# Second layer: pairs from tile 2 on and to the end, combined activations directly behind the norm, squares beside the pairs

## The chip, the core and the metric

The kernel runs on one core of one Trainium2 chip. The metric is the device time of one execution in microseconds (us). Engines are named as the profile names them: PE (TensorE matmuls), PEld (TensorE weight loads, beside PE), DVE (VectorE), ACT (ScalarE), POOL (GpSimd) and SP (SyncE, which here only starts transfers). Each engine works through its own instructions in order; an instruction that waits for another engine holds up everything behind it on its own.

## What is computed

A trunk of two layers over 1024 tokens of 1024 channels, all in fp32. The first layer mixes tokens by a convolution, the second by trailing means (pool); each is followed by a SwiGLU feed-forward part (FFN) with 2816 hidden channels. Cut to what matters:

```python
def swiglu_ffn(h, w_gate, w_up, w_down):
    return (jax.nn.silu(h @ w_gate) * (h @ w_up)) @ w_down

for i in range(DEPTH):                       # DEPTH = 2
    h = modulate(rms_norm(x, norm_mix_g[i]), sh_m, sc_m)
    y = conformer_conv(...) if i % 2 == 0 else multiscale_pool(...)
    x = x + (1.0 + g_m)[:, None, :] * y
    h = modulate(rms_norm(x, norm_ffn_g[i]), sh_f, sc_f)
    y = swiglu_ffn(h, ffn_w_gate[i], ffn_w_up[i], ffn_w_down[i])
    x = x + (1.0 + g_f)[:, None, :] * y
return rms_norm(x, final_g)
```

## The kernel before

**Tiling.** Tokens are split into two chunks of 512, A (tiles named x_0_*) and B (x_1_*), with channels on the 128 partitions, so x of a chunk is 8 tiles of 128x512. The hidden channels of the FFN are 22 tiles of 128 (NF = 22), called f-tiles. fp32 products are made from high and low parts: `hhi`/`hlo` for activations, a cast for the high part and the remainder for the low one, and weights in the same way; each product is three matmuls (high·high, high·low, low·high).

**Plain f-tiles** (`ffn_p1`): gate and then up of one f-tile, 8 × 3 = 24 matmuls of 512 columns each. **Downs** (`ffn_p2`): for two f-tiles, 8 output tiles of 6 matmuls, each added to x by DVE (`update`).

**Pairs** (`ffn_pair`, L1133): gate (or up) of two f-tiles at once, in the manner of Strassen, with 7 quarter products where the plain way has 8. Each is a `quad` of 12 matmuls of 256 columns. Four quads use weights or activations that are sums: the weight sums s1 to s4 (`Pair.prepare`; cast to `shi` and `slo` tiles) and the activation sums t1 to t4 (`combined`; `thi` and `tlo`), called T. A pair unit writes two PSUM banks: bank a takes quads w11, s2, s3 and w22 one on top of the other in its left half, bank e takes s1 and s4 in its right and w12 in its left half. Since the running sum in a is needed at three stages, ACT copies it away after w11 and again after s2, and the next quad into a waits for that copy. In all but the first pair of a stage, four slots of downs of the pair before it (6 matmuls of 512 columns each) stand between the quads. The core of the unit:

```python
quad(a[:, :H], w11, b11, True)
S_.copy(r[:, LEFT], a[:, :H])
quad(right, s1, t1, True)
S_.copy(q[:, RIGHT], right)
down()
quad(a[:, :H], s2, t2, False)
S_.copy(r[:, RIGHT], a[:, :H])
quad(left, w12, b21, False)
down()
quad(a[:, :H], s3, t3, False)
```

(S_ is ACT, V_ is DVE, G_ is POOL.)

**Which f-tiles are pairs.** `ffn_mixed` (L1210) makes the first PLAIN = 4 f-tiles plain, the f-tiles up to UNTIL[stage] as pairs, and the rest plain. UNTIL is 16 for the first layer's B and the second layer's A, and 20 for the second layer's B. It hands back three lists: `before` (the plain start), `pairs`, and `rest`, the last of which is the last downs of the stage. `alone` does the four slots of downs that are left behind the last pair, `ending` the last downs of all with the final norm of B.

**Order of the stages** at the end of the trunk: the FFN of B in the first layer beside the pool of A, the FFN of A in the second layer beside the pool of B, the FFN of B in the second layer beside `final` of A (the last norm of A and its output). The last downs of a stage are put behind the first plain f-tile of the next, which works on the other chunk.

**What sets the order.** PE's order is that of the units. The other work beside it is done by tasks (`put` starts one, `need` finishes it) that are moved on in `pace()`, as far as planned clocks of DVE and POOL allow; a task that isn't urgent has a low priority in the scheduler, which decides where its instructions go among those of DVE, ACT and POOL. Such tasks are `combined` (T), `pool_stats` (squares of x with `sum_sq`, their sum, and the reciprocal root `rstd` for the pool's norm) and `final`. Weights are loaded ahead by `ahead()` in `run_units`, which counts the slots that loaded and used weights hold.

Of the kernel before, what the change touches and what calls it, by code (L numbers as in the profile page):

```python
# [21 lines left out]
NF = F // P  # L22
# [32 lines left out]
WARM = (22, 10, 6)  # L55
EARLY_X = 4
PREPARED = 120
PLAIN = 4
UNTIL = (16, 16, 20)
OUT_AT = 6  # L60
DELAY = {"stats": 2.75, "spread": 1.5}
DELAY_BEHIND = {"stats": 8, "spread": 4}
# [53 lines left out]
def trunk(ctx, tc, xT, c, vec, ada, adan, w1, w2, wgu, wdn, wpl, wph, out):  # L116
# [59 lines left out]
    forced = [False]  # L176

    def step(t, e):
        behind[0] = not t.urgent
        before = {k: engines[k].spent for k in "VG"}  # L180
        with tc.high_priority(offset=0 if t.urgent else -LATER):
            moved = t.step(e)
        behind[0] = False
        for k in "VG":
            clock[k] += (stretch[0] - 1) * (engines[k].spent - before[k])
        return moved
# [313 lines left out]
                    self.acc = temp(ch.n, "acc", 2)  # L500
                V_.tensor_tensor(self.acc, was, sq, op=ADD)

    def sum_sq(srcs, n):
        acc = None
        for s in srcs:
            if acc is None:
                acc = temp(n, "acc", 2)
                S_.activation(acc, s, AF.Square)
            else:
                sq = temp(n)  # L510
                S_.activation(sq, s, AF.Square)
                V_.tensor_tensor(acc, acc, sq, op=ADD)
            yield
        return acc
# [37 lines left out]

    units = []
    reserve = [0]

    def unit(emit, *weights):
        units.append((weights, emit))
# [10 lines left out]
    def run_units(cap, early):  # L568

        queue = [w for ws, _ in units for w in ws]  # L570
        loaded = list(early)
        del queue[: len(early)]
        used = [0]
        cost = lambda w: 4 if isinstance(w, Pair) else 2

        def ahead():
            held = sum(cost(w) for w in loaded) + used[0] + reserve[0]
            while queue and (held + cost(queue[0]) <= cap or not loaded or isinstance(queue[0], Pair) and all(
                    isinstance(w, Pair) and w.made is not None for w in loaded)):
                w = queue.pop(0)  # L580
                held += cost(w)
                if isinstance(w, Own):
                    loaded.append(load_weight(w.src, low=V_))
                else:
                    loaded.append(w.load() if isinstance(w, Pair) else load_weight(w, summed=True))
                if len(loaded) > 1:
                    break

        st["ahead"] = ahead
        for ws, emit in units:  # L590
            took = [0]

            def take():
                ahead()
                w = loaded.pop(0)
                took[0] += cost(w)
                used[0] += cost(w)
                return w
            emit(take)
            used[0] -= took[0]  # L600
            ahead()
            pace()

# [526 lines left out]
                self.load(d // 2 + 1)  # L1130
            pace()

    def ffn_pair(ch, l, me, following, downs, later):  # L1133


        def emit(take):
            wt = take()
            wt.prepare()
            ws = wt.made
            h, T = st["h", ch.i], st["T", ch.i]  # L1140
            half = KT // 2
            b11 = [(hi[:, LEFT], lo[:, LEFT]) for hi, lo in h[:half]]
            b21 = [(hi[:, LEFT], lo[:, LEFT]) for hi, lo in h[half:]]
            b22 = [(hi[:, RIGHT], lo[:, RIGHT]) for hi, lo in h[half:]]
            t1, t2, t3, t4 = ([T[k][j] for k in range(half)] for j in range(4))
# [12 lines left out]
            r, q = temp(ch.n), temp(ch.n)  # L1158
            quad(a[:, :H], w11, b11, True)
            S_.copy(r[:, LEFT], a[:, :H])  # L1160
            quad(right, s1, t1, True)
            S_.copy(q[:, RIGHT], right)
            pace()
            down()
            quad(a[:, :H], s2, t2, False)
            S_.copy(r[:, RIGHT], a[:, :H])
            if following is not None and hasattr(following, "raws"):
                following.prepare()
                st["ahead"]()
            quad(left, w12, b21, False)  # L1170
            pace()
            down()
            quad(a[:, :H], s3, t3, False)
            V_.tensor_tensor(q[:, RIGHT], q[:, RIGHT], a[:, :H], op=ADD)
            quad(right, s4, b22, False)
            V_.tensor_tensor(r, r, e, op=ADD)
            if later is not None:
                later.load(later.dps[0])
            pace()
            down()  # L1180
            quad(a[:, :H], w22, t4, False)
            if me.which == 0:
                sg = st["sg", ch.i] = [window(ch.n, "sg") for _ in range(2)]
                S_.activation(sg[0], r, AF.Silu)
                S_.activation(sg[1][:, RIGHT], q[:, RIGHT], AF.Silu, scale=-1.0)
                S_.activation(sg[1][:, LEFT], a[:, :H], AF.Silu, scale=-1.0)
            else:
                sg = st["sg", ch.i]
                V_.tensor_tensor(r, r, sg[0], op=MUL)
                V_.scalar_tensor_tensor(q[:, RIGHT], q[:, RIGHT], -1.0, sg[1][:, RIGHT], op0=MUL, op1=MUL)  # L1190
                V_.scalar_tensor_tensor(q[:, LEFT], a[:, :H], -1.0, sg[1][:, LEFT], op0=MUL, op1=MUL)
                for i, t in enumerate((r, q)):
                    hi, lo = st["g", ch.i, me.f + i] = gslots(ch)
# [13 lines left out]
            reserve[0] = 0  # L1207
        return emit, ()

    def ffn_mixed(ch, l, until, at_end=False):  # L1210

        before = []
        for f in range(0, PLAIN, 2):
# [3 lines left out]
        mates = [Pair(ch, l, f, which) for f in range(PLAIN, until, 2) for which in range(2)]  # L1217
        mine, theirs = [None] * len(mates), []
        for i, f in enumerate(range(PLAIN - 2, until - 2, 2)):
# [9 lines left out]
        for i, me in enumerate(mates):  # L1229
            if i + 1 == len(mates):  # L1230
                paired.append((lambda take: reserve.__setitem__(0, 2), ()))
            paired.append(ffn_pair(ch, l, me, mates[i + 1] if i + 1 < len(mates) else None, mine[i], (mine + [last])[i + 1]))
        paired.append((lambda take: last.load(last.dps[1]), ()))
        rest = ffn(ch, l, True, at_end, until, ffn_p2(ch, l, [until - 2, until - 1], True))
        rest[1:1] = [alone(last)]
        if not at_end:
# [61 lines left out]
        return emit, tuple(wdn[l, f] for f in fs)  # L1298

    def final(ch):  # L1300
        acc = yield from sum_sq(x[ch.i], ch.n)
        rstd = yield from mean_rsqrt(acc, ch.n, True)
        for k in range(KT):
            xs = x[ch.i][k]
# [214 lines left out]
    unit(lambda take: stretch.__setitem__(0, 1.0))  # L1519


    def pool_stats(ch):
        acc = yield from sum_sq(x[ch.i], ch.n)
# [18 lines left out]
    def pooled(us, ch, out_at):  # L1542
# [13 lines left out]
        need(("nf", ch.i))  # L1556
        unit(lambda take: st.__setitem__(("h", ch.i), st["hn", ch.i]))

    def paired(ch, us):
        need(("T", ch.i))  # L1560
        add(us)

    before, pairs, rest = ffn_mixed(B, 0, UNTIL[0])
    put(("T", 1), lambda: combined(B))
    add(before[:2])
    put(("stats", 0), lambda: pool_stats(A))
# [1 line left out]
    need(("stats", 0))  # L1568
    paired(B, pairs)
    pooled(rest[:-1], A, OUT_AT)  # L1570
    before, pairs, rest_a = ffn_mixed(A, 1, UNTIL[1])
    add(before[:1] + rest[-1:])
    put(("T", 0), lambda: combined(A))
    add(before[1:2])
    put(("stats", 1), lambda: pool_stats(B))
    add(before[2:])
    need(("stats", 1))
    paired(A, pairs)
    pooled(rest_a[:-1], B, OUT_AT)
    before, pairs, rest = ffn_mixed(B, 1, UNTIL[2], True)  # L1580
    add(before[:1] + rest_a[-1:])
    put(("T", 1), lambda: combined(B))
    add(before[1:])
    put("final_a", lambda: final(A))
    paired(B, pairs)
    add(rest)
# [54 lines left out]
```

## Time and profile before

| | us |
|---|---|
| median of 3 runs | 1807.41 |
| lowest and highest | 1804.94, 1807.71 |
| profiled execution, whole | 1807.51 |
| span of its profile | 1805.6 |

All times of the trace come from this one profiled execution; a start time counts from the beginning of its span. In the second half the stages lie as follows:

| stretch of the span, us | what PE does |
|---|---|
| 1063.6 to 1074.5 | second layer, A: plain f-tile 0 |
| 1074.5 to 1085.4 | first layer, B: last downs |
| 1085.4 to 1129.8 | A: plain f-tiles 1 to 3, downs of 0 and 1 |
| 1129.8 to 1312 | A: pairs |
| 1430 to 1493 | second layer, B: the same start, with A's last downs |
| 1493 to 1740 | B: pairs |
| 1740 to the end | B: plain f-tiles 20 and 21, last downs, final norm |

How to read the views: a row of instructions shows start and length in us, engine, line and operation, the tile written and those read with their shapes, and in brackets the idle time just before with the instruction that ended it. ACT and DVE show line 110 and PE line 132 for all work, since helpers there record every instruction; so tiles tell the work apart (`gate`, `up` and `dn` are PSUM banks, `t` scratch tiles, `raw` and `w` weights as loaded and as split).

### The profile page before, as it was taken

The numbers are of one execution on the slowest core, as the hardware profiler recorded it, in microseconds if no ns is written. First come the engines' busy times: TensorE is split into PE (matmuls) and PEld (weight loads), VectorE is DVE, ScalarE is ACT, GpSimd is POOL, SyncE is SP. The second block draws the span as 40 slices with busy tenths as digits, with TensorE's granted clock in tenths as the row PEclk, the third lists the DMA queues.
The fourth block names the chain that finished last, engine by engine and source line by source line (L and its number), as shares of the span: only waits on it lengthen the run. The fifth ranks groups of instructions, "written<-read, shape, count | busy, mean of one in ns | idle before, by whom it ended". The sixth has DMA issues, their size and how long they took to land.

```text
span 1805.6 us, 26287 instructions
## 1 busy us (share of the span) xinstructions
PE 1775.1 (98%) x9788; PEld 1525.8 (85%) x9788; DVE 1324.6 (73%) x2139; ACT 1023.5 (57%) x1593; POOL 567.9 (31%) x614
## 2 busy tenths in 40 slices
PE   9999998999999999999999999999999999999997
PEld 7777777888888888899998888999988889999986
DVE  7689846978775328989979569787695578887745
ACT  4766665776746455555553546555445446555543
POOL 0389723887734121211117212110161111111111
PEclk9999999999999999999999999999999999999998
DMA  9968676998988998877765866555548766655562
GB/s 301 287 180 263 171 165 169 236 224 202 243 201 206 236 221 195 231 205 205 200 194 128 206 155 167 147 126 139 146 117 205 162 141 164 182 140 141 128 141 71
DMA packets 112786, 331.21 MB, mean 183 GB/s; under 512 B 11153, under 2 KB 21521, under 8 KB 112658
## 3 DMA queue, kind: packets, MB, share of 16 engines
q1 hardware_dynamic: 76656, 222.56, 37.5%
q0 software_dynamic: 34848, 105.92, 32.8%
q8 instruction: 77, 1.26, 0.3%
q10 hardware_dynamic: 1154, 1.05, 0.2%
q14 instruction: 51, 0.42, 0.1%
HBM read 325.29 MB, written 4.19 MB: 182 GB/s over the span
## 4 chain that ended last, share of the span: by engine, by line
PE 92%; DVE 2%; issue 2%; DMA 1%; ACT 1%; POOL 1%; POOLq 0%; SPq 0%; ACTq 0%; DVEq 0%
PE dn L132 26%; PE gate L132 25%; PE up L132 25%; PE y L132 5%; PE a L132 3%; PE g L132 2%; PE first L132 2%; PE idle L132 1%; PE ada L132 1%; ACT w L110 1%; PE rstd L132 1%; DMA adaw<-in_adan_dram 0%; ACT t L110 0%; DMA w<-in_w_dram 0%; PE var L132 0%
## 5 line engine op out<-in xcount | busy, mean ns | idle before, releaser
L132 PE MATMUL dn<-ghi,w 128*128 128x512 f32 (+1 forms) x1440 | 466.8, 387 | 0.6 <-ACT t L110 0.6
L110 ACT CAST w<-raw 128x1024 fp32r<-128x1024 f32 (+1 forms) x390 | 319.8, 824 | 174.8 <-PE dn L132 78.9
L110 ACT ACTIVATE w<-raw 128x1024 fp32r<-128x1024 f32 (+1 forms) x242 | 221.9, 917 | 264.5 <-PE dn L132 80.5
L110 DVE SCALAR_TENSOR_TENSOR x<-dn,gains,x 128x512 f32<-128x512 f32 (+1 forms) x360 | 262.3, 735 | 71.2 <-PE dn L132 66.1
L132 PEld LDWEIGHTS dn<-ghi,w 128*128 128x128 f32 x1440 | 269.0, 188 | 51.5 <-ACT t L110 1.0
L132 PE MATMUL gate<-hhi,w 128*128 128x512 f32 (+1 forms) x1088 | 310.4, 359 | 0.0
L132 PE MATMUL up<-hhi,w 128*128 128x512 f32 (+1 forms) x1088 | 310.1, 358 | 0.0
L132 PE MATMUL dn<-glo,w 128*128 128x512 f32 (+1 forms) x720 | 278.6, 387 | 0.1
L110 POOL TENSOR_TENSOR pa<-pa,pr 128x512 f32<-128x512 f32 x174 | 240.6, 1481 | 41.4 <-ACT pr L110 38.3
L1084 POOL DMA_DIRECT2D w<-in_wgu_dram x80 | 69.7, 875 | 491.9 <-ACT w L110 155.2
L132 PEld LDWEIGHTS gate<-hhi,w 128*128 128x128 f32 x1088 | 196.7, 189 | 31.9 <-ACT hhi L110 0.4
L132 PEld LDWEIGHTS up<-hhi,w 128*128 128x128 f32 x1088 | 196.7, 189 | 30.6
L132 PE MATMUL gate<-hlo,w 128*128 128x512 f32 (+1 forms) x544 | 194.8, 358 | 0.0
L132 PE MATMUL up<-hlo,w 128*128 128x512 f32 (+1 forms) x544 | 194.6, 358 | 0.0
L424 POOL DMA_DIRECT2D w<-in_wgu_dram x92 | 82.4, 896 | 335.5 <-ACT w L110 300.8
L110 DVE SCALAR_TENSOR_TENSOR ca<-u,vecs,ca 128x512 f32<-128x512 f32 x246 | 171.7, 748 | 0.9
L110 DVE TENSOR_TENSOR t<-t,up 128x512 f32<-128x512 f32 (+1 forms) x88 | 54.9, 625 | 153.4 <-PE up L132 150.9
L132 PEld LDWEIGHTS dn<-glo,w 128*128 128x128 f32 x720 | 135.7, 189 | 22.0 <-POOL glo L110 0.6
L110 DVE TENSOR_TENSOR w<-raw,w 128x512 fp32r<-128x512 f32 (+1 forms) x148 | 118.0, 803 | 32.2 <-ACT w L110 29.1
L110 ACT ACTIVATE pr<-u,vecs 128x512 f32<-128x512 f32 x174 | 118.5, 717 | 26.3 <-POOL pa L110 17.2
L132 PEld LDWEIGHTS gate<-hlo,w 128*128 128x128 f32 x544 | 102.6, 189 | 15.7 <-DVE hlo L110 0.2
L132 PEld LDWEIGHTS up<-hlo,w 128*128 128x128 f32 x544 | 102.7, 189 | 15.5
(192 smaller groups left out, 3345.5 us busy)
## 6 DMA issues: line engine op xcount, KB each, us to landing
raw<-in_wgu_dram SPq DMA_DIRECT2D x176, 512.0 KB, 4.9
w<-in_wgu_dram POOLq DMA_DIRECT2D x92, 512.0 KB, 8.1
raw<-in_wdn_dram SPq DMA_DIRECT2D x88, 512.0 KB, 5.3
adaw<-in_ada_dram SPq DMA_DIRECT2D x64, 512.0 KB, 5.0
raw<-in_w_dram SPq DMA_DIRECT2D x42, 512.0 KB, 6.5
w<-in_wgu_dram POOLq DMA_DIRECT2D x80, 256.0 KB, 5.6
w<-in_wdn_dram POOLq DMA_DIRECT2D x34, 512.0 KB, 8.1
adaw<-in_adan_dram SPq DMA_DIRECT2D x32, 512.0 KB, 6.1
```

The source lines that it names most:

```text
L110: self.last = self.order(getattr(self.eng, name)(out, *args, **kw))
L132: last_mm[0] = nc.tensor.matmul(out, lhsT, rhs, start=start, stop=stop, **kw).ins.name
L424: order(nc.gpsimd.dma_start(as_src(lo), src, accum_op=ADD))
L1084: order(nc.gpsimd.dma_start(lo, src, accum_op=ADD))
```

## The change

1. In the second layer the plain start has 2 f-tiles in place of 4, for both chunks, and B's pairs go on to f-tile 21. That makes six pair units more: A's f-tiles 2 and 3, B's 2 and 3, and B's 20 and 21, a gate and an up unit each. Behind B's last pair stand only `alone` and `ending`.
2. T of the second layer is started right behind the first plain f-tile, ahead of the other chunk's last downs, and at the priority of urgent work (`put_eager`).
3. `pool_stats(B)` is started behind the second plain f-tile, and finished after A's pairs, where it was finished before them. Its sum, and that of `final`, go into the tile `cact`, which is free by then.
4. In the first pair of each of the three stages quad w12 comes second, so that s2 and s3 follow each other.
5. The slots that weights hold are counted down in the last pair.

```diff
-PLAIN = 4
-UNTIL = (16, 16, 20)
+PLAIN = (4, 2, 2)
+UNTIL = (16, 16, 22)
...
-        behind[0] = not t.urgent
+        at_once = t.urgent or getattr(t, "eager", False)
+        behind[0] = not at_once
-        with tc.high_priority(offset=0 if t.urgent else -LATER):
+        with tc.high_priority(offset=0 if at_once else -LATER):
...
-    def sum_sq(srcs, n):
+    def sum_sq(srcs, n, into=None):
-                acc = temp(n, "acc", 2)
+                acc = temp(n, "acc", 2) if into is None else into[:, :n]
...
             quad(a[:, :H], w11, b11, True)
             S_.copy(r[:, LEFT], a[:, :H])
-            quad(right, s1, t1, True)
+            if plain_first:
+                quad(left, w12, b21, True)
+            quad(right, s1, t1, not plain_first)
...
-            quad(left, w12, b21, False)
+            if not plain_first:
+                quad(left, w12, b21, False)
+            if following is None:
+                used[0] -= 2
+                st["ahead"]()
...
+        if until == NF:
+            return before, paired, [alone(last), ending(ch, l, [until - 2, until - 1])]
...
     def final(ch):
-        acc = yield from sum_sq(x[ch.i], ch.n)
+        acc = yield from sum_sq(x[ch.i], ch.n, cact)
...
+    def put_eager(name, gen):
+        def emit(take):
+            T[name] = Task(gen(), False, 0)
+            T[name].eager = True
+            finish_some(T[name])
+        unit(emit)
+
+    def finish_some(t):
+        for _ in range(2):
+            step(t, "V")
...
-    add(before[:1] + rest[-1:])
-    put(("T", 0), lambda: combined(A))
-    add(before[1:2])
-    put(("stats", 1), lambda: pool_stats(B))
-    add(before[2:])
+    add(before[:1])
+    put_eager(("T", 0), lambda: combined(A))
+    add(rest[-1:] + before[1:])
+    put(("stats", 1), lambda: pool_stats(B, cact))
+    paired(A, pairs)
     need(("stats", 1))
-    paired(A, pairs)
...
-    add(before[:1] + rest_a[-1:])
-    put(("T", 1), lambda: combined(B))
-    add(before[1:])
+    add(before[:1])
+    put_eager(("T", 1), lambda: combined(B))
+    add(rest_a[-1:] + before[1:])
     put("final_a", lambda: final(A))
     paired(B, pairs)
```

Two places in the compiled order. The first is ACT at the first pair of A in the second layer (the pair's gate unit). `t<-gate` is a copy out of a PSUM bank of the pair, `shi` are sums of weights, `w<-raw` weights of later units, and `ghi` the product of an earlier plain f-tile; brackets show whose semaphores an instruction waits for. Before:

```order
L110 CAST w_10603<-raw_10385 128x512 [waits DMAHW6_49,DMASW0_49]
L110 CAST w_10663<-raw_10385 128x512 [waits PE_49]
L110 CAST w_10679<-raw_10561 128x512 [waits DMAHW1_49,DMASW1_49,PE_49]
L110 CAST ghi_10437<-t_10439 128x512 [waits DVE_49]
L110 COPY t_10485<-gate_10483 128x256 [waits PE_49,Activation_49]
L110 CAST w_10680<-raw_10561 128x512 [waits Activation_49]
L110 ACTIVATE w_10680<-raw_10561 128x512
L110 CAST shi_10539<-acc_10537 128x512 [waits PE_49]
L110 COPY t_10486<-gate_10484 128x256 [waits PE_49]
L110 CAST shi_10545<-ny_10543 128x512 [waits PE_49]
L110 COPY t_10485<-gate_10483 128x256 [waits PE_49]
```

The same place in the changed kernel; `x_3_88` to `x_5_90` are tiles of B, whose squares `pool_stats(B)` takes:

```order
L110 CAST w_10438<-raw_10332 128x512 [waits DMAHW4_49,DMASW6_49,PE_49]
L110 ACTIVATE w_10438<-raw_10332 128x512
L110 CAST ghi_10178<-t_10180 128x512 [waits DVE_49]
L110 CAST shi_10308<-acc_10306 128x512 [waits PE_49]
L110 ACTIVATE t_10196<-x_3_88 128x512 [waits DVE_49]
L110 ACTIVATE t_10199<-x_4_89 128x512 [waits DVE_49]
L110 ACTIVATE t_10202<-x_5_90 128x512 [waits DVE_49]
L110 COPY t_10242<-gate_10240 128x256 [waits Pool_49]
L110 COPY t_10243<-gate_10241 128x256 [waits DVE_49,PE_49]
L110 CAST shi_10314<-ny_10312 128x512 [waits PE_49]
L110 COPY t_10242<-gate_10240 128x256 [waits PE_49]
```

The first copy out of the gate bank stood ahead of the cast of `shi`; now it stands behind it and behind three squares. The cast of shi_10308 waits for the last matmul of quad s1, which is the last reader of the slot that it writes.

The second place is PE in the same pair unit. Shown are the matmuls at the borders of its first quads: the last of w11, the first and last of the next ones, and so on. Before (gate_10483 is bank a, gate_10484 is bank e):

```order
L132 MATMUL gate_10483<-hhi_9536,w_10448 128x256
L132 MATMUL gate_10484<-thi_10074,shi_10461 128x256
L132 MATMUL gate_10484<-thi_10223,slo_10462 128x256
L132 MATMUL gate_10483<-thi_10074,shi_10467 128x256
L132 MATMUL gate_10483<-thi_10223,slo_10468 128x256
L132 MATMUL gate_10484<-hhi_9538,w_10449 128x256
L132 MATMUL gate_10484<-hhi_9544,w_10449 128x256
L132 MATMUL gate_10483<-thi_10078,shi_10473 128x256
```

And in the changed kernel (gate_10240 is a, gate_10241 is e):

```order
L132 MATMUL gate_10240<-hhi_9536,w_10205 128x256
L132 MATMUL gate_10241<-hhi_9538,w_10206 128x256
L132 MATMUL gate_10241<-hhi_9544,w_10206 128x256
L132 MATMUL gate_10241<-thi_9989,shi_10218 128x256
L132 MATMUL gate_10241<-thi_10158,slo_10219 128x256
L132 MATMUL gate_10240<-thi_9989,shi_10224 128x256
L132 MATMUL gate_10240<-thi_10158,slo_10225 128x256
L132 MATMUL gate_10240<-thi_9993,shi_10230 128x256
```

The quads came in the order w11, s1, s2, w12, s3; now it is w11, w12, s1, s2, s3, so that between the quads s2 and s3, which both accumulate into bank a, nothing else is left.

More of the change, by code (lines that the diff above doesn't have):

```diff
@@ L554, in trunk @@
     reserve = [0]
+    used = [0]
     def unit(emit, *weights):
@@ L572, in run_units @@
         del queue[: len(early)]
-        used = [0]
         cost = lambda w: 4 if isinstance(w, Pair) else 2
@@ L600, in run_units @@
             used[0] -= took[0]
+            used[0] = max(used[0], 0)
             ahead()
@@ L1131, in slot, with ffn_pair @@
             pace()
-    def ffn_pair(ch, l, me, following, downs, later):
+    def ffn_pair(ch, l, me, following, downs, later, plain_first=False):
         def emit(take):
@@ L1208, in alone, with ffn_mixed @@
         return emit, ()
-    def ffn_mixed(ch, l, until, at_end=False):
+    def ffn_mixed(ch, l, plain, until, at_end=False):
         before = []
-        for f in range(0, PLAIN, 2):
+        for f in range(0, plain, 2):
             before += [ffn_p1(ch, l, f, True, False), ffn_p1(ch, l, f + 1, True, False)]
@@ L1216, in ffn_mixed @@
                 before.insert(-1, own(ffn_p2(ch, l, [f - 2, f - 1], True)))
-        mates = [Pair(ch, l, f, which) for f in range(PLAIN, until, 2) for which in range(2)]
+        mates = [Pair(ch, l, f, which) for f in range(plain, until, 2) for which in range(2)]
         mine, theirs = [None] * len(mates), []
-        for i, f in enumerate(range(PLAIN - 2, until - 2, 2)):
+        for i, f in enumerate(range(plain - 2, until - 2, 2)):
             first, second = Downs(ch, l, (f, f + 1), (0, 1)), Downs(ch, l, (f, f + 1), (2, 3))
@@ L1231, in ffn_mixed @@
                 paired.append((lambda take: reserve.__setitem__(0, 2), ()))
-            paired.append(ffn_pair(ch, l, me, mates[i + 1] if i + 1 < len(mates) else None, mine[i], (mine + [last])[i + 1]))
+            paired.append(ffn_pair(ch, l, me, mates[i + 1] if i + 1 < len(mates) else None, mine[i], (mine + [last])[i + 1], i == 0))
         paired.append((lambda take: last.load(last.dps[1]), ()))
+        if until == NF:
+            return before, paired, [alone(last), ending(ch, l, [until - 2, until - 1])]
         rest = ffn(ch, l, True, at_end, until, ffn_p2(ch, l, [until - 2, until - 1], True))
@@ L1519, in trunk, with pool_stats @@
     unit(lambda take: stretch.__setitem__(0, 1.0))
-    def pool_stats(ch):
-        acc = yield from sum_sq(x[ch.i], ch.n)
+    def pool_stats(ch, into=None):
+        acc = yield from sum_sq(x[ch.i], ch.n, into)
         steps = st["spread", ch.i] = mean_rsqrt(acc, ch.n, True, "col2")
@@ L1561, in paired @@
         add(us)
-    before, pairs, rest = ffn_mixed(B, 0, UNTIL[0])
+    before, pairs, rest = ffn_mixed(B, 0, PLAIN[0], UNTIL[0])
     put(("T", 1), lambda: combined(B))
@@ L1570, in trunk @@
     pooled(rest[:-1], A, OUT_AT)
-    before, pairs, rest_a = ffn_mixed(A, 1, UNTIL[1])
-    add(before[:1] + rest[-1:])
-    put(("T", 0), lambda: combined(A))
-    add(before[1:2])
-    put(("stats", 1), lambda: pool_stats(B))
-    add(before[2:])
+    before, pairs, rest_a = ffn_mixed(A, 1, PLAIN[1], UNTIL[1])
+    add(before[:1])
[3 more added lines that the diff above has]
+    paired(A, pairs)
     need(("stats", 1))
-    paired(A, pairs)
     pooled(rest_a[:-1], B, OUT_AT)
-    before, pairs, rest = ffn_mixed(B, 1, UNTIL[2], True)
-    add(before[:1] + rest_a[-1:])
-    put(("T", 1), lambda: combined(B))
-    add(before[1:])
+    before, pairs, rest = ffn_mixed(B, 1, PLAIN[2], UNTIL[2], True)
+    add(before[:1])
+    put_eager(("T", 1), lambda: combined(B))
+    add(rest_a[-1:] + before[1:])
     put("final_a", lambda: final(A))
```

## The prediction

> **What bounds the kernel now.** I read the summary lines first, then the shares of the chain of work that ended last.
>
> ```profile
> span 1805.6 us, 26287 instructions
> PE 1775.1 (98%) x9788; PEld 1525.8 (85%) x9788; DVE 1324.6 (73%) x2139; ACT 1023.5 (57%) x1593; POOL 567.9 (31%) x614
> PE 92%; DVE 2%; issue 2%; DMA 1%; ACT 1%; POOL 1%; POOLq 0%; SPq 0%; ACTq 0%; DVEq 0%
> ```
>
> PE is busy for 98% of the span and holds 92% of the chain. The profiled execution took 1807.51 us, its span and 1.91 us around it; the median of the three runs is 1807.41, so sums against 1807.51 hold for both. What happens where the change works is in the view of stretches: start:end in us, length, busy time with count of PE, PEld, DVE, ACT, POOL, then granted clock, DMA share, GB/s. The first row is the plain start of A's second-layer FFN, the second its pairs, the third and fourth the same of B, the fifth the end.
>
> ```profile
> 1060.00:1130.00 70.00, 70.00 (x316) 58.15 (x315) 52.59 (x95) 35.42 (x54) 11.95 (x12) 1.00 0.66 162
> 1130.00:1312.00 182.00, 182.00 (x1282) 170.64 (x1281) 137.17 (x217) 100.94 (x192) 21.36 (x31) 1.00 0.53 136
> 1430.00:1493.00 63.00, 63.00 (x280) 52.16 (x280) 39.16 (x67) 29.58 (x44) 9.23 (x10) 1.00 0.62 146
> 1493.00:1740.00 247.00, 245.41 (x1721) 228.96 (x1720) 196.11 (x326) 136.97 (x264) 26.99 (x31) 1.00 0.57 151
> 1740.00:1806.00 66.00, 52.91 (x282) 45.54 (x280) 30.14 (x78) 25.90 (x50) 12.06 (x16) 0.93 0.44 96
> ```
>
> PE does not pause in the first three, at full clock. ACT is busy for 35.42 of 70 and 100.94 of 182 us, so it has room on average, and DMA is less busy in pairs (0.53) than in plain tiles (0.66): six more pair units bring no bandwidth limit. From 630 us to the end PE waits for hardly anything (total, times, longest):
>
> ```profile
> PE rstd L132 <- DVE col L110: 6.4, 3, 2.7
> PE dn L132 <- ACT t L110: 0.6, 1, 0.6
> ```
>
> So there is little waiting to remove. A gain must come from fewer or shorter matmuls, and whatever makes PE wait in the pairs is paid in full.
>
> **The change part by part.** *Six more pair units* (A: tiles 2 and 3; B: 2, 3, 20, 21; gate and up each). The chain in order of time (start, us, work) has both forms:
>
> ```profile
> 1074.47 10.88 PE dn L132 x48
> 1085.36 5.44 PE gate L132 x24
> 1090.80 5.44 PE up L132 x24
> 1096.23 5.44 PE gate L132 x24
> ...
> 1129.78 10.01 PE gate L132 x84
> 1139.78 2.87 PE up L132 x24
> ...
> 1155.33 2.86 PE gate L132 x24
> ...
> 1170.87 2.86 PE up L132 x24
> ```
>
> Two plain gates are 48 matmuls of 512 columns, 2 × 5.44 = 10.88 us. The first pair unit, 84 matmuls of 256 columns with no downs between, takes 10.01. A later unit goes from 1155.33 to 1170.87, 15.54 us, with four slots of downs of 6 matmuls each, which at 5.44/24 are 5.44 us and are needed in either form; 10.10 is left. A unit so saves 10.88 − 10.10 = 0.78 us (0.87 by the first unit). **Six save 4.7 us** (4.7 to 5.2).
>
> [...]
>
> *The copies of the first pair, displaced in ACT's queue.* Each pair unit copies half of its first bank away (COPY t<-gate) before quad s2 may accumulate into it. ACT before, at A's first pair, and ahead of it its four waits since 1085 (brackets: idle time, releaser):
>
> ```profile
> 1090.83 1.06 ACT L110 CAST w<-raw 128x1024 fp32r<-128x1024 f32 x1 [0.83 <-PE gate L132]
> 1093.62 0.62 ACT L110 CAST thi<-tf 128x512 fp32r<-128x512 f32 x1 [1.22 <-DVE tf L110]
> 1096.27 1.06 ACT L110 CAST w<-raw 128x1024 fp32r<-128x1024 f32 x1 [2.03 <-PE up L132]
> 1101.48 1.06 ACT L110 ACTIVATE w<-raw 128x1024 fp32r<-128x1024 f32 x1 [0.55 <-PE gate L132]
> ...
> 1131.30 0.37 ACT L110 COPY t<-gate 128x256 f32<-128x256 f32 x1
> 1131.57 0.63 ACT L110 CAST w<-raw 128x512 fp32r<-128x512 f32 x1
> 1132.10 0.63 ACT L110 ACTIVATE w<-raw 128x512 fp32r<-128x512 f32 x1
> 1132.62 0.60 ACT L110 CAST shi<-acc 128x512 fp32r<-128x512 f32 x1
> 1133.13 0.37 ACT L110 COPY t<-gate 128x256 f32<-128x256 f32 x1
> 1133.99 0.62 ACT L110 CAST shi<-ny 128x512 fp32r<-128x512 f32 x1 [0.48 <-PE gate L132]
> 1134.52 0.37 ACT L110 COPY t<-gate 128x256 f32<-128x256 f32 x1
> ```
>
> There the copy starts at 1131.30, right behind the first quad (1129.78 plus 12 of 84 × 10.01 = 1.43 us, so 1131.21), and s2 finds it done. In the changed order the copy stands behind a cast shi that waits for quad s1 to release its slot, and behind three squares of the other chunk's norm. One ACT instruction of 512 columns follows another by 0.53 us (1131.57, 1132.10, 1132.62). At best, then, the copy ends 4 × 0.53 + 0.37 = 2.5 us after s1's end.
>
> Whether ACT is there by then I read off its order. The pairs of A now follow its second plain tile (the gate and up of 1085.36 and 1090.80), so they start at 1096.23 on the old time axis: up to there PE's work is the same in both. Three quads of 1.43 later, at 1100.5, PE wants s2. The first cast that waits for the second tile's last matmuls can start at 1096.3; the copy stands 14 instructions behind it. 14 × 0.53 = 7.4, so it starts at 1103.7 and ends at 1104.1: **PE waits 3.6 us**. If one of those 14 meets a wait as long as the longest of ACT's four before, 2.03, it is 5.6. B's first pair has the same sequence in ACT's order, again with 14 instructions between, and final(A)'s squares in the place of pool_stats(B)'s. So 2 × 3.6 = **7.2 us** (5.0 to 11.2). Before, B's squares ran ahead of its pairs:
>
> ```profile
> 1488.69 1.66 ACT L110 ACTIVATE t<-x 128x512 f32<-128x512 f32 x3
> ...
> 1491.81 0.64 ACT L110 ACTIVATE t<-x 128x512 f32<-128x512 f32 x1
> 1494.52 0.37 ACT L110 COPY t<-gate 128x256 f32<-128x256 f32 x1 [2.07 <-PE gate L132]
> ```
>
> ACT there stood idle for 2.07 us until the first quad was done: that slack is what the change uses up.
>
> *Quad w12 in second place* (in the first pair of three stages: B in the first layer, A and B in the second). Before, the order is w11, s1, s2, w12, s3; now it is w11, w12, s1, s2, s3. What stood between s2 and s3 is gone, and a second copy must fit there: s3 accumulates into the half bank that s2 has just filled. In the rows above the cast at 1133.99 is released by s2's last matmuls and the copy behind it ends at 1134.52 + 0.37 = 1134.89. Before, w12 (1.43 us) covered these 0.9 us; now nothing does. 3 × 0.9 = **2.7 us** (1.2, with the copy's 0.37 alone, to 2.7). What it buys, 1.43 us more between s1's operands and the pair's start, has no wait to remove in the rows before.
>
> *Combined activations ahead of the first layer's last downs.* The same instructions earlier in DVE's queue. s1 needs the last of them by 1100.2; the cast for it stands on ACT ahead of the one that waits for the second tile, so DVE can finish two 0.63 us steps later, before 1098.5. Cost nothing; if that cover went, PE would wait for it in s1 and the copy would be as much less late, so the two don't add. The eight updates of x that they overtake release banks only.
>
> *Squares into cact, squares needed after the pairs, the reserve count.* The same number of instructions; the norm's rstd for the pool is wanted only after the pairs, 180 us later, so nothing is late. *The end of B*: the last pair's product is followed by four downs, 5.44 us, of the pair before it, as cover for making its g tiles.
>
> ```profile
> L110 DVE TENSOR_TENSOR t<-t,up 128x512 f32<-128x512 f32 (+1 forms) x88 | 54.9, 625 | 153.4 <-PE up L132 150.9
> ```
>
> That takes about four DVE steps of 0.63 and one ACT cast of 0.62, 3.1 us. Hidden, and the tail behind it (the fifth stretch) stays.
>
> **Sum**: 1807.5 − 4.7 + 7.2 + 2.7 = **1812.7 us**, 0.29% more than before. By the bounds: 1807.5 − 5.2 + 5.0 + 1.2 = 1808.5, and 1807.5 − 4.7 + 11.2 + 2.7 = 1816.7.
>
> **The rivals.** *The stall costs clock too.* After one wait early in the kernel the granted clock fell to half. PE's row at its end (start, us, and the wait in brackets):
>
> ```profile
> 213.11 1.19 PE L132 MATMUL mean<-acc,ones 128*128 128x512 f32 x1 [3.72 <-DVE acc L110]
> ```
>
> The view of stretches there (start:end, length, PE busy and count, granted clock, DMA share, GB/s):
>
> ```profile
> 211.00:212.00 1.00, 0.00 (x0) 1.00 1.01 201
> 212.00:213.00 1.00, 0.00 (x0) 0.70 0.85 328
> 214.00:215.00 1.00, 1.00 (x3) 0.50 0.75 147
> 218.00:219.00 1.00, 1.00 (x4) 0.50 0.00 0
> 219.00:220.00 1.00, 1.00 (x5) 0.88 0.00 0
> ```
>
> From 213.11 to about 219.2 PE ran at 0.50, which lost half of 6.1 us, 3.0. The wait of 2.7 us (the rstd row) near the end is shorter, and the stall forecast here, 3.6, is just under the 3.72 that did it. One site so gives 1815.7, both 1818.7. [...]
>
> *The copies are only partly late*: ACT is ahead of its 0.53 us steps, or PE's wait in s1 takes part of them; the floor above, 1808.5 to 1810.5. For it speaks that ACT has half its time free; against it that the 14 instructions stand in one queue behind one event.
>
> *Faster*: if the unit's 0.78 us come in full and the copies are on time (by ACT reaching them before s1 ends, which needs the shi slot to come free earlier than by s1's last matmul), the new waits vanish: 1807.5 − 4.7 = 1802.8, and 1801.2 if the 1.6 us that PE waits in B's pairs (247.00 − 245.41) go as well. It decides at a copy that ends by 1100.5; the order of ACT speaks against it.
>
> *That it does not do what it says*: the compiled order has 504 matmuls of 256 columns more and 288 of 512 fewer, six units' worth, so the pairs are there. No chance for it.
>
> **How the numbers follow.** Forecast (1810.5 to 1815) 50%; partly late (1806 to 1810.5) 25%; clock or still later copies (1815 to 1819) 17%; faster 8%. The range of 8 in 10 goes from 1806.0 to 1818.0: below it is the faster case, above it the stall that costs clock at both sites. About 0.2% (3.6 us) can be told from no change here; that puts "same" at 1803.9 to 1811.1. It holds the partly late case and the lowest end of the forecast's, 27%. What is left of the forecast and the clock case make slower, 65%; faster 8%.
>
> **What would show it.** PE's waits by releaser: a new row "gate <- ACT t" of about 9.9 us in 5 pieces, the longest 3.6. In ACT's rows at both first pairs: shi, three squares, then the copy, with PE idle before s2. The chain: rows of a gate pair of 2 × 5.44 replaced by 10.1. The granted clock in both first pairs: 1.00 if the forecast is right, 0.50 for some 6 us if the clock rival is. Wrong would be: no wait on t at all (faster), or waits in later pair units (ACT then lags throughout).

## The result, and the profile after

| | before | after |
|---|---|---|
| median, us (4 runs each) | 1807.56 | 1820.38 |
| lowest and highest | 1804.94, 1807.78 | 1819.61, 1821.69 |
| profiled execution, whole (span) | 1807.51 (1805.6) | 1819.61 (1817.6) |

The changed kernel is slower: the ratio is 1.0073, with a 95% interval of 1.0061 to 1.0085. The forecast was 1812.7 us with a range up to 1818.0. The time moved the way that was forecast, but by +12.8 us where +5.2 was forecast.

The summary lines of the changed kernel:

```profile
span 1817.6 us, 26874 instructions
PE 1775.3 (98%) x10004; PEld 1537.3 (85%) x10004; DVE 1369.1 (75%) x2217; ACT 1038.1 (57%) x1648; POOL 563.0 (31%) x611
```

PE's busy time is what it was (1775.1 us before), although six pair units should have taken 4.7 us off it. That is the first hint that some of its work ran slower. What PE waited for from 640 us on (total, times, longest):

```profile
PE gate L132 <- ACT t L110: 12.1, 5, 6.4
PE rstd L132 <- DVE col L110: 5.9, 3, 2.5
PE dn L132 <- ACT t L110: 0.6, 1, 0.6
```

The first row is new, in five pieces as forecast: one in the first layer's first pair of B, two each in the second layer's first pairs of A and B. PE's rows at these places (start, length, and in brackets the wait just before):

```profile
770.99 0.39 PE L132 MATMUL gate<-thi,shi 128*128 128x256 f32 x1 [0.86 <-ACT t L110]
1106.96 0.58 PE L132 MATMUL gate<-thi,shi 128*128 128x256 f32 x1 [6.39 <-ACT t L110]
1110.65 0.58 PE L132 MATMUL gate<-thi,shi 128*128 128x256 f32 x1 [0.77 <-ACT t L110]
1477.46 0.58 PE L132 MATMUL gate<-thi,shi 128*128 128x256 f32 x1 [3.36 <-ACT t L110]
1481.16 0.39 PE L132 MATMUL gate<-thi,shi 128*128 128x256 f32 x1 [0.77 <-ACT t L110]
```

The short ones, before quad s3, are near the 0.9 us forecast. Of the long ones, before quad s2, B's is 3.36 (forecast 3.6) and A's is 6.39. ACT's rows at A's first pair say why A differs:

```profile
1102.01 0.61 ACT L110 CAST shi<-acc 128x512 fp32r<-128x512 f32 x1
1102.53 1.67 ACT L110 ACTIVATE t<-x 128x512 f32<-128x512 f32 x3
1106.54 0.37 ACT L110 COPY t<-gate 128x256 f32<-128x256 f32 x1 [2.34 <-POOL glo L110]
```

The cast, the three squares and the copy follow each other as in the compiled order, but the copy then stands still for 2.34 us until POOL has made `glo` of the second plain f-tile: `glo` reads the scratch tile that the copy is to write. In B the same copy starts at once:

```profile
1475.36 1.67 ACT L110 ACTIVATE t<-x 128x512 f32<-128x512 f32 x3
1477.04 0.37 ACT L110 COPY t<-gate 128x256 f32<-128x256 f32 x1
```

POOL's rows at both places:

```profile
1102.56 3.95 POOL L110 TENSOR_TENSOR glo<-t,ghi 128x512 fp32r<-128x512 f32 x1
...
1475.39 1.61 POOL L110 TENSOR_TENSOR glo<-t,ghi 128x512 fp32r<-128x512 f32 x1
```

The same instruction took 3.95 us in A and 1.61 in B, where it ended (1477.00) just as ACT was through with the squares. So 2.34 of A's 6.39 us are POOL's; the rest, and all of B's wait, is ACT's queue.

The second cost is the clock. Stretches of A's first pair (start:end, length, PE busy and count, granted clock, DMA share, GB/s), around the end of the long wait at 1106.96:

```profile
1104.00:1105.00 1.00, 0.00 (x0) 1.00 0.92 207
1105.00:1106.00 1.00, 0.00 (x0) 0.53 1.04 231
1112.00:1113.00 1.00, 1.00 (x7) 0.50 0.00 0
1115.00:1116.00 1.00, 1.00 (x9) 0.85 0.00 0
```

And the rest of both first gate units as a whole, A's and B's:

```profile
1106.96:1117.26 10.30, 9.53 (x50) 0.60 0.13 18
1477.46:1485.69 8.23, 7.46 (x50) 0.81 0.32 64
```

Before, both first pairs ran at 1.00. Taken from the clock alone, 9.53 us of work at 0.60 lost 9.53 × 0.40 = 3.8 us and 7.46 at 0.81 lost 1.4. That is an estimate, and a little high: the same matmuls, from the first of s2 to the first of the up unit behind, can be timed directly. The first two rows are those of A and B in the changed kernel, the third is A in a run below (`glo` on DVE, s2 from 1104.66 on) whose clock stayed at 1.00:

```profile
1117.10 0.28 PE L132 MATMUL up<-hhi,w 128*128 128x256 f32 x1
1485.52 0.28 PE L132 MATMUL up<-hhi,w 128*128 128x256 f32 x1
...
1111.61 0.28 PE L132 MATMUL up<-hhi,w 128*128 128x256 f32 x1
```

That is 10.14 and 8.06 us where full clock takes 6.95, so the half clock cost 3.2 us in A and 1.1 in B. With the forecast's 4.7 for the six units and the measured size of the other terms, the sum of the prediction reads 1807.5 − 4.7 + (6.4 + 3.4) + 2.4 + (3.2 + 1.1) = 1819.3 us, or 1820.2 with 3.8 and 1.4; the profiled execution took 1819.61. The experiments test these terms.

### The profile page after: what moved, and what is told of

Same layout as the page of the kernel before. It is cut to its first block, busy times and chain, and to the rows that moved or that the text cites. A ratio compares the mean times of both kernels' runs of the same rounds, so it can differ in the third digit from the quotient of the medians.

```text
span 1817.6 us, 26874 instructions
## 1 busy us (share of the span) xinstructions
PE 1775.3 (98%) x10004; PEld 1537.3 (85%) x10004; DVE 1369.1 (75%) x2217; ACT 1038.1 (57%) x1648; POOL 563.0 (31%) x611
## 5 line engine op out<-in xcount | busy, mean ns | idle before, releaser
L110 ACT CAST w<-raw 128x512 fp32r<-128x512 f32 (+1 forms) x402 | 320.1, 799 | 169.4 <-PE up L132 72.0
L110 ACT ACTIVATE w<-raw 128x1024 fp32r<-128x1024 f32 (+1 forms) x240 | 214.6, 894 | 220.9 <-PE dn L132 64.5
L132 PE MATMUL up<-hhi,w 128*128 128x512 f32 (+1 forms) x1040 | 289.3, 352 | 0.0
L132 PE MATMUL gate<-hhi,w 128*128 128x512 f32 (+1 forms) x1040 | 289.1, 353 | 0.0
L132 PEld LDWEIGHTS gate<-hhi,w 128*128 128x128 f32 x1040 | 186.4, 189 | 28.2 <-ACT hhi L110 0.4
L132 PEld LDWEIGHTS up<-hhi,w 128*128 128x128 f32 x1040 | 186.7, 189 | 26.9
L132 PE MATMUL gate<-hlo,w 128*128 128x512 f32 (+1 forms) x520 | 183.1, 352 | 0.0
L132 PE MATMUL up<-hlo,w 128*128 128x512 f32 (+1 forms) x520 | 182.9, 352 | 0.0
L110 DVE TENSOR_TENSOR t<-t,up 128x256 f32<-128x256 f32 (+1 forms) x88 | 54.3, 617 | 113.9 <-PE up L132 111.5
L110 ACT CAST shi<-ny 128x512 fp32r<-128x512 f32 x92 | 57.1, 620 | 114.2 <-PE gate L132 57.0
```

The lines of the kernel that those rows point to most:

```text
L110: self.last = self.order(getattr(self.eng, name)(out, *args, **kw))
L132: last_mm[0] = nc.tensor.matmul(out, lhsT, rhs, start=start, stop=stop, **kw).ins.name
```

## The experiments

Each was timed in three rounds against the kernel before, on the same chip. The gate units meant are the first pair units of A and B in the second layer.

### The quads in their old order

```diff
-            paired.append(ffn_pair(..., (mine + [last])[i + 1], i == 0))
+            paired.append(ffn_pair(..., (mine + [last])[i + 1]))
```

> The changed kernel with one edit undone: quad w12 back between s2 and s3 in the first pairs (w11, s1, s2, w12, s3), all else as changed. Theory (ACT gets to the first pair's copy too late, because a shi cast, three squares and the release of a scratch tile stand ahead of it): the three short waits between s2 and s3 go (0.86 + 0.77 + 0.77 = 2.4 us), but s2 now wants the copy one quad, 1.43 us, earlier while the copy comes no sooner, so the two long waits grow to some 7.8 and 4.8 us: 1820.4 - 2.4 + 2.9 = 1820.9, 1819 to 1823. Rival (the order of the quads is what costs): the long waits vanish with it and the time falls to 1803 to 1808.

Measured: 1820.97 us, ratio to before 1.0080 (1.0065 to 1.0095). Its waits:

```profile
PE gate L132 <- ACT t L110: 14.0, 2, 7.3
```

The three short waits are gone and the two long ones have grown, to 7.3 and 6.7. So the place of w12 is not what costs. The copy is asked for 1.43 us earlier here. In A it is waited for 0.9 us longer, so there it comes at nearly the same time (0.5 us earlier). In B the wait grew by 3.4, more than the order explains: POOL's `glo` took 3.90 us there in place of 1.61, and the last square ahead of the copy stood still for it:

```profile
1473.53 3.90 POOL L110 TENSOR_TENSOR glo<-t,ghi 128x512 fp32r<-128x512 f32 x1 [0.37 <-ACT ghi L110]
1477.47 0.63 ACT L110 ACTIVATE t<-x 128x512 f32<-128x512 f32 x1 [2.90 <-POOL glo L110]
```

So B's short wait in the changed kernel hung on a short `glo`. The time is as the theory had it, but not in its parts: the two waits together are 1.4 longer than forecast, and the clock loses less in A (a mean of 0.84 over the 10.75 us behind the wait; in B 0.79 over 10.59).

### The squares one unit later

```diff
-    put(("stats", 1), lambda: pool_stats(B, cact))
-    paired(A, pairs)
+    need(("T", 0))
+    add(pairs[:2])
+    put(("stats", 1), lambda: pool_stats(B, cact))
+    add(pairs[2:])
...
-    put("final_a", lambda: final(A))
-    paired(B, pairs)
+    need(("T", 1))
+    add(pairs[:2])
+    put("final_a", lambda: final(A))
+    add(pairs[2:])
```

> The changed kernel with the squares (pool_stats of B, final of A) started one unit later, behind the first gate unit of the pairs; nothing else differs. Theory: with the squares away the first copy stands right behind its quad, the waits of 6.4 and 3.4 us go and with them the half clock behind both (some 3.4 and 1.5 us); the short waits between s2 and s3 of about 0.8 stay: 1820.4 - 9.8 - 4.9 = 1805.7, 1804 to 1808, PE at full granted clock in both first pairs. Rival (the quads' order, or the combined activations started early, cost the time): 1817 to 1821. Rival (the squares only move the wait on): long waits on t in the second unit, 1812 or more.

Measured: 1808.09 us, ratio 1.0002 (0.9991 to 1.0012). Twelve of the 12.8 us are back, and neither rival holds. Waits of the profiled execution, and below it one of the stretches behind the longest of them:

```profile
PE gate L132 <- ACT t L110: 4.0, 3, 2.3
...
1105.00:1106.00 1.00, 1.00 (x7) 0.50 0.84 164
```

The forecast was 2.4 us too low. A's wait before s3 is 2.3, not 0.8: between the first copy and the second ACT had four weight instructions, ghi, two shi and the copy of bank e to do, and in this order of the quads PE has nothing else until then. Behind it the clock fell to half here too.

### Both at once: squares later, quads in their old order

> Both at once: squares started behind the first gate unit, and quad w12 back in its old place. Theory: the long waits go by the first edit and the three short ones by the second, as long as the combined activations reach quad s1 one quad earlier: the six units' gain shows nearly in full, 1820.4 - 9.8 - 4.9 - 2.4 = 1803.3, 1802 to 1806, below the kernel before. Rival (w12 in second place is needed, since the combined activations come too late without it): a wait of PE on thi or tlo before s1 of 1 to 3 us at each of the two places, 1805 to 1810.

Measured: 1803.59 us, ratio 0.9977 (0.9966 to 0.9989): faster than the kernel before, as forecast. The list of waits has no row on `t` before a gate any more:

```profile
PE rstd L132 <- DVE col L110: 6.2, 3, 2.7
PE var L132 <- DVE acc L110: 0.6, 1, 0.6
PE dn L132 <- ACT t L110: 0.6, 1, 0.6
```

With the squares away, w12 between s2 and s3 covers the second copy as it did before the change, and the combined activations reach s1 in time without w12 ahead of it. The same kernel was run again beside the last two experiments:

> Squares one unit later and w12 back, again, for comparison on the same chip: 1803.6 measured before, 1802 to 1805 expected by every theory.

Measured: 1802.88 us, ratio 0.9974 (0.9965 to 0.9983). In this profiled execution one wait of 0.5 us on `tlo` shows before a gate, far below the 1 to 3 us of the rival.

### The pairs alone, without the edits on order

The kernel before, with PLAIN = (4, 2, 2) and UNTIL = (16, 16, 22) and nothing else.

> The kernel before with the first edit alone: pairs from f-tile 2 in the second layer and to the end in B; combined activations, squares and quads as before. Theory: the six units save 4.7 us, but squares and combined activations no longer have two plain f-tiles to run in, and both must be through before the first pair: ACT reaches A's first copy late (before: it follows the seventh square and the last two thi casts), PE waits 3 to 8 us at A's first pair and less at B's, with some clock lost: 1806 to 1815. Rival (it is the edits on order that cost, not the lack of room on ACT): no new wait, 1802.8.

Measured: 1829.03 us, ratio 1.0118 (1.0103 to 1.0133), far above both forecasts. The theory named the wrong wait. The worst wait is not for the copy:

```profile
1112.08 0.37 PE L132 MATMUL var<-ones,acc 128*128 128x1 f32 x1 [16.77 <-DVE acc L110]
```

Since the squares must be through before the pairs, their sum (a few small matmuls) stands in PE's order ahead of the first pair. With one plain f-tile instead of three between the last downs and that place, DVE is 16.8 us late with it. PE's other new waits are for `thi` and `tlo`, 4.8 us in all at B's first pair. So the parts of the change that move the squares behind the pairs and start the combined activations early are needed for the longer pairs, at least together; neither was tried alone. What costs in the changed kernel is not that they were moved, but how the squares and the copies beside them get into each other's way.

### The longer end alone

The kernel before, with UNTIL = (16, 16, 22).

> The kernel before with only B's pairs of the second layer going on to the end (f-tiles 20 and 21 as pairs, two units more); plain starts, squares and quads as before. Theory (a pair unit saves 0.78 to 0.87 us and the making of the last g tiles lies behind four slots of downs): 1.6 to 1.7 us less than before, 1805.7, with no new wait at the end. Rival (the last downs wait for the g tiles of the last unit): a wait of PE's dn of 1 to 3 us near 1765, 1807 to 1809.

Measured: 1806.11 us beside 1807.14 of the kernel before, ratio 0.9995 (0.9985 to 1.0004): by the times alone too small to tell. Between two matmuls that both traces have, early in B's pairs and in the ending, the distance can be read. Before:

```profile
1556.86 0.38 PE L132 MATMUL rstd<-ident,col 128*128 128x128 f32 x1 [1.32 <-DVE col L110]
...
1787.62 0.27 PE L132 MATMUL var<-ones,acc 128*128 128x1 f32 x1 [0.57 <-DVE acc L110]
```

In this experiment:

```profile
1557.01 0.38 PE L132 MATMUL rstd<-ident,col 128*128 128x128 f32 x1 [1.32 <-DVE col L110]
...
1786.21 0.27 PE L132 MATMUL var<-ones,acc 128*128 128x1 f32 x1 [0.57 <-DVE acc L110]
```

230.76 us became 229.20: 1.56 less, two units at 0.78, and the wait at both ends is the same in both. The rival, a wait for the last g tiles, is out: the list of waits has no such row.

### glo on DVE

```diff
-            either(ch.n).tensor_tensor(lo, t, hi.bitcast(F32), op=SUB)
+            (V_ if l and f == 1 else either(ch.n)).tensor_tensor(lo, t, hi.bitcast(F32), op=SUB)
```

> The changed kernel with the remainder glo of the second plain f-tile (second layer) made on DVE instead of POOL; in the compiled order the first copy then also has two squares ahead of it in place of three. Theory (A's wait is 3 us longer than B's because the copy's scratch tile is let go by POOL's glo, which took 3.95 us in A and 1.61 in B): A's wait falls from 6.4 to about 3.5 and B's from 3.4 to 2.9, A's time at half clock shortens, 1820.4 - 3.4 - 0.5 to 2 = 1814.5 to 1816.5. Rival (DVE or ACT are the ones that are late and POOL only comes last by chance): A's wait stays above 5.5, 1819 to 1821.

Measured: 1818.28 us, ratio 1.0064 (1.0047 to 1.0081). In the profiled execution A's long wait is 3.43, as the theory had it, and B's 3.14:

```profile
1104.66 0.39 PE L132 MATMUL gate<-thi,shi 128*128 128x256 f32 x1 [3.43 <-ACT t L110]
```

So POOL's glo, with the one square that the compiled order then has less ahead of the copy, was 3 us of A's wait. The time gained less than forecast in most executions: the profiled one took 1812.62 us, at a clock of 1.00 behind A's wait, the other three 1817.7 to 1819.9 with a lower mean clock over the span (0.986 to 0.989, where the profiled one had 0.992). It looks as if the same wait may or may not cost clock; the three have no trace that would show where theirs went.

### Idle matmuls inside the waits

```diff
             quad(right, s1, t1, not plain_first)
+            if plain_first and l:
+                planned = clock["PE"]
+                warm(12)
+                clock["PE"] = planned
```

> The changed kernel with 12 idle matmuls (128x128, fp32, into a spare bank, read by nobody; about 2.6 us) put behind quad s1 in the two first pairs of the second layer, inside the two long waits. Theory (part of the loss is the half clock that follows the long waits: 10.3 us at a mean of 0.60 in A and 8.2 us at 0.81 in B, 3.8 and 1.4 us): the waits on t shrink by 2.6 us each to 3.8 and 0.8, the copies come no earlier, and the clock stays at 1.00 in B and for the most part in A: 1820.4 - 1.4 - 1.9 to 3.8 = 1815 to 1817. Rival (the clock falls for another reason than PE's idleness): the granted clock in both pairs as in the changed kernel, 1820 or more.

Measured: 1818.84 us, ratio 1.0063 (1.0048 to 1.0078). The stretches behind the two waits, A's in two rows, B's in one:

```profile
1108.43:1114.00 5.57, 4.81 (x24) 0.58 0.12 21
1114.00:1118.50 4.50, 4.50 (x31) 0.76 0.00 0
1478.28:1486.00 7.72, 6.86 (x55) 1.00 0.38 78
```

In B 0.68 us of waiting was left in place of 3.36, and the clock stayed at 1.00 where the changed kernel had a mean of 0.81: in this execution the half clock there went together with PE's idleness. In A 3.95 us were left and the clock fell all the same, so the 1.9 to 3.8 us forecast for A did not come. The median is 1.5 us below the changed kernel's, of the size of B's 1.1 to 1.4. The agreement is not to be pressed: in the profiled execution the short wait in the first layer, which the edit does not touch, was 1.93 us in place of 0.86.

### The copies in another scratch ring

```diff
-            r, q = temp(ch.n), temp(ch.n)
+            own_tile = plain_first and l
+            r, q = (window(ch.n, "r"), window(ch.n, "q")) if own_tile else (temp(ch.n), temp(ch.n))
```

> The changed kernel with the copies of the first gate unit of A and B (second layer) put into tiles of another scratch ring (the one of 3 tiles that sg uses), so that they no longer wait for one of the 4 scratch tiles that the squares take in turn; the squares stay where they are. Theory (the copy stands behind the squares because it waits for a scratch tile in their ring, and ACT works in order): in the compiled order the first copy moves right behind quad w11, so the waits of 6.4 and 3.4 us before s2 go, while a wait of 0.9 to 1.5 us before s3 stays at each first pair, behind shi, a square and the second copy: 1820.4 - 12.1 + 0.9 + 2 x 1.3 - 5.2 = 1806.6, up to 1810 if one of these waits costs clock as the 2.3 us in e2 did. Rival (ACT is behind with its work altogether, whatever the tile): the sum of the waits on t stays above 8 us, 1815 or more.

Measured: 1808.89 us, ratio 1.0004 (0.9994 to 1.0013). The same squares run beside the same unit, but the long waits before s2 are gone: the first copy now starts ahead of four weight instructions, `ghi` and four of the squares, 1.8 us after quad w11 (1097.70 to 1099.13 in A):

```profile
1100.97 0.37 ACT L110 COPY r<-gate 128x256 f32<-128x256 f32 x1
```

So the copy was late for the sake of its tile, not because ACT had too much to do. What is left:

```profile
PE gate L132 <- ACT r L110: 3.8, 2, 2.5
PE gate L132 <- DVE q L110: 1.0, 1, 1.0
PE gate L132 <- ACT t L110: 0.9, 1, 0.9
```

The 3.8 us are the second copies before s3, 2.5 of them in A, much as with the squares later (2.3), and behind A's the clock fell there too (a mean of 0.83 from 1101 to 1111 us; in B it was 1.00 from 1469 to 1479). Both put the time above the forecast, by 2.3 us, within the bound set for such a loss. The 1.0 us come later in B's unit, the 0.9 are the first layer's. With w12 back between s2 and s3 as well:

> As the run before, and quad w12 back between s2 and s3 in all three first pairs, squares still beside the first pair. Theory: no wait on t over 0.5 us is left, the six units' gain shows: 1820.4 - 12.1 - 5.2 = 1803.1, 1801 to 1806, about as with the squares one unit later. Rival (squares beside the first unit cost by themselves, through ACT's and DVE's time): waits on t, thi or tlo of 2 us or more, 1807 or more.

Measured: 1802.82 us, ratio 0.9973 (0.9962 to 0.9984); the squares beside the first unit then cost nothing that the times show. Waits on the copies:

```profile
PE gate L132 <- ACT q L110: 1.0, 2, 0.7
PE gate L132 <- DVE tlo L110: 0.3, 1, 0.3
```

POOL's `glo` is slow here too (4.33 us in A), and PE does not wait for it, now that the first copies take no tile of the ring that it reads from:

```profile
1101.17 4.33 POOL L110 TENSOR_TENSOR glo<-t,ghi 128x512 fp32r<-128x512 f32 x1 [0.62 <-ACT ghi L110]
```

This version and the one with the squares later beat both kernels, by 4.9 and 4.8 us against the kernel before on the same chip; between the two there is no difference to tell.

## Why the prediction was right and wrong, point by point

- **Six pair units save 4.7 us**: right. Two units alone gave 1.56 us in the trace, and with the waits gone all six show 4.8 to 4.9 (3.7 in the first run of the version with the squares later and w12 back).
- **The copies come late, 3.6 us at each first pair**: the mechanism and B's size were right (3.36), A's was not (6.39). The prediction counted ACT's 14 instructions and let the copy start after the last of them. It left out that the copy also waits for the tile it writes, which the compiled order shows in its row (it waits for POOL, and for no other engine). POOL's glo took 3.95 us there and held the copy up for 2.34; with glo on DVE the wait was 3.43. B's agreement rests on glo being short there: with the quads in their old order it was not, and B's wait was 6.7, of which the order explains 1.43. And the place of the copy in ACT's order had the same root: it stood behind the squares since it took its turn in the ring of 4 scratch tiles that they use, as the run with the copies in another ring shows.
- **Quads s2 and s3 next to each other cost 0.9 us in three pairs**: right (0.86, 0.77, 0.77), and gone with the old order of the quads.
- **The clock holds**: this is the step that failed most. The forecast's sum has no term for it. It took a stall of 3.6 us to be just under what costs clock, by one wait of 3.72 that had done so, and gave the case that it does, together with still later copies, 17%. That a wait must come near 3.72 us to cost clock was its estimate from that one wait, and the runs show no such limit: one of 2.32 was followed by half clock, one of 3.43 was not. In the changed kernel the clock fell to half at both places (0.50 in A from 1112 to 1113 us, in B from 1478 to 1480), which cost 4.3 us by the rows and 5.2 by the clock's share. That is the larger part of the 6.9 us by which the forecast lies below the profiled execution (7.7 below the median); A's longer wait, 2.8, is the other, and B's wait and the short ones were together 0.5 shorter than forecast. The rival with clock loss at both sites, 1818.7, came close, in part by luck: it had 3.0 us at each site, where A lost 3.2 and B 1.1, and it lacked A's longer wait. The trace before held a warning that the prediction passed over. It named the wait of 2.7 us near the end only as shorter than 3.72, but the clock fell to half within that wait, which came 1.1 us after another of 2.37 and ended at 1797.37 (stretches of the kernel before, columns as above):

```profile
1796.00:1797.00 1.00, 0.00 (x0) 0.60 0.39 131
1797.00:1798.00 1.00, 0.63 (x3) 0.50 0.64 218
```

- **Combined activations early, squares in cact, the end of B at no cost**: right as far as no wait on thi, tlo or the last downs shows in the changed kernel. What was not seen is that the early start and the late squares are needed, at least together: without them the kernel with the same pairs was 21.8 us slower than the kernel before.

Not tried: the early start and the late squares each by itself, the count of weight slots in the last pair by itself, and any more pairs in the first layer.

## What to carry to other kernels

When PE has nothing but a chain of small copies between two products, look at the row of the copy in the compiled order and ask for every engine it waits for, the tile it writes included: a scratch tile in a ring shared with side work makes the side work part of the chain (2.34 of the 6.39 us of A's wait here). Put the copies of the critical unit into tiles of their own, or start the side work one unit later, and keep some independent product between two that accumulate into the same bank (here w12 took away the three waits of 0.77 to 0.86 us). In this kernel new waits of PE of 2.3 us and more in most cases cost half clock on top, 3.2 and 1.1 us in the changed kernel, so give such a wait a price for that in the sum, unless runs show otherwise.

## What the runs showed of the hardware that was not expected

- **Clock.** A single wait of PE of 2.32 us was followed by half clock (squares later, 1105 to 1106 us), and one of 2.49 too (copies in another ring). One of 3.14 (glo on DVE, B) and one of 3.36 were followed by a mean of 0.81 over some 8 us, while one of 3.43 was followed by 8.3 us at 1.00 (glo on DVE, A). The row of that one:

```profile
1104.66:1113.00 8.34, 7.47 (x60) 1.00 0.55 116
```

  So the length of a wait alone does not settle it; what does, no run here shows.
- **POOL beside DVE.** In A, while glo took 3.95 us, DVE's rows follow each other without a gap:

```profile
1102.25 0.71 DVE L110 TENSOR_TENSOR cact<-cact,t 128x512 f32<-128x512 f32 x1
1102.85 0.71 DVE L110 TENSOR_TENSOR slo<-acc,shi 128x512 fp32r<-128x512 f32 x1
1103.45 0.71 DVE L110 TENSOR_TENSOR cact<-cact,t 128x512 f32<-128x512 f32 x1
1104.05 0.71 DVE L110 TENSOR_TENSOR acc<-raw 128x512 f32<-128x512 f32 x1
1104.65 2.40 DVE L110 TENSOR_TENSOR cact<-cact,t 128x512 f32<-128x512 f32 x2
```

  In B DVE stood idle for 0.27 us, and glo started within that gap:

```profile
1475.49 2.08 DVE L110 TENSOR_TENSOR slo<-acc,shi 128x512 fp32r<-128x512 f32 x1 [0.27 <-ACT shi L110]
```

  There glo took 1.61 and DVE's slo 2.08, where the slo of A's rows took 0.71. With the quads in their old order glo took 3.90 in B. From 640 us on the changed kernel has twelve glo of this shape, of 1.29 to 3.95 us. What DVE does beside a glo was not varied by itself, so why their times differ is not shown.
